# A decoder layer on one core: the MLP's order planned anew, result tiles stored by fewer DMAs

## The chip, the cores and the metric

The kernel runs on one core of a Trainium2 chip. The metric is device time of one execution in microseconds. Three runs before the change took 558.32, 559.50 and 561.14 us, so the median is 559.5 us. The core's engines are TensorE (PE, with its weight loads as PEld), VectorE (DVE), ScalarE (ACT), GpSimd (POOL) and SyncE (SP, which here issues nearly all DMAs). Each engine takes its instructions strictly in the order of the program.

## The reference, cut to what matters

One decoder layer over 512 tokens of width 1024, in float32:

```
xn   = rms_norm(h, g_mix_norm);  proj = xn @ w_in
attn = moba_attention(q, k, v);  conv = conformer_conv(u, ...)
h    = h + concat(attn, conv) @ w_out
hn   = rms_norm(h, g_mlp_norm)
ff   = square(relu(hn @ w_mlp_in))       # 1024 -> 4096
h    = h + ff @ w_mlp_out                # 4096 -> 1024
out  = rms_norm(h, g_final)
```

The change concerns the last four lines: the MLP and the final norm.

## The kernel before, in words

TensorE keeps float32 accuracy by splitting both operands into a high part (rounded, on ACT) and a low part (the rest, `x - high`, a subtraction on DVE or POOL), and multiplying three times: high*high, high*low, low*high (`mm3`, L268 to L270).

The MLP runs in four chunks (c = 0 to 3) of 1024 hidden columns. A chunk has two phases.

- *Hidden phase*: eight blocks of 24 matmuls (`hidden`, tile `ff`). Each needs a 128x1024 tile of w1, loaded as `raw`, and split into `wh` (ACT) and `wl` (kind `mw`). The result goes through `relu_square` (ACT makes `rl`, DVE makes `F`).
- *Product phase*: the second matrix product is done by Strassen's scheme: seven products of half-size blocks instead of eight, in the order 3, 6, 4, 2, 1, 5, 7 (`spread`, `product`, tiles `m`; 24 matmuls each, in two halves j = 0 and 1). Each product needs an operand `O[m]` made of `F` (a sum or difference into a `temp`, kind `ms`, then high part `ma..h` on ACT and low part `mal`), and two weight tiles `B[m]` made of w2 blocks (a sum or difference, kind `mt`, into a tile `t` or `r`, then `wh`, and `wl` of kind `mb`). Product 1's weights are built in place in the tiles of product 2's (`s1 = sums("mt1", r11, ...)` needs `low_of(2)`): the sum for product 1 can start only when the low part of product 2's weights has been taken. Each product is added from PSUM to the residual `xr` by DVE (`add_to`, L1092), up to four 128x512 additions a product.

The sums, differences and low parts are all 128x1024 operations with two inputs in SBUF (L1058, L1066). A chunk has 44 of them: 8 `mw`, 14 `mb`, 10 `mt`, 7 `mal`, 5 `ms`. The table `ON` says on which engines each kind may stand; a kind that is not in it may stand on either.

At the end each of four 128-token tiles is normed: ACT squares and sums, POOL does the small scalar steps and the power (`fr`), one half of the tile is multiplied by g_fin first and scaled later (`mfo`, `mfy`), the other in one operation (`mfz`), and each half is stored by its own DMA from SP.

The order on each engine is not written by hand. Class `Plan` simulates the engines with costs in us, and at each turn emits the step that can start first, with a bias by kind (`BIAS`) between steps that are about even. It has one `port` that POOL operations and DVE operations marked `shared` (two SBUF inputs) hold in turn: such a step is taken to start only when the port is free.

Of the kernel before, what the change touches and what calls it, by code (L numbers as in the profile page):

```python
# [13 lines left out]
AF = mybir.ActivationFunctionType  # L14
# [22 lines left out]
    "mal": ("dve",), "ms1": ("dve",), "ms5": ("dve",), "ms6": ("dve",), "ms7": ("pool",), "mt1": ("pool",),  # L37
    "mt3": ("pool",), "mt6": ("pool",), "mt7": ("dve",),
# [31 lines left out]
class Plan:  # L70
# [32 lines left out]
    def run(self):  # L103
# [8 lines left out]
        while ready:  # L112
            best, first = [], {}
            for s in ready:
# [56 lines left out]
def hybrid_layer(ctx: ExitStack, tc: tile.TileContext, x, pack, w_in, w_out, g_mlp, w1, w2, g_fin, out):  # L171
# [882 lines left out]
    def low_parts(kind, lo, x, hi, needs, uses):  # L1054
# [5 lines left out]
        l = plan.step(kind, either(kind), 0, fn, needs=needs, uses=uses, shared=True)  # L1060
        return l

    def combine(kind, out, a, b, op, needs, uses):
# [84 lines left out]

    def final_ssq(t, cols, ready, half, final):
# [7 lines left out]

# [247 lines left out]
```

## Time and profile before

| | |
|---|---|
| median of three runs | 559.5 us |
| profiled execution | 559.28 us, of which the traced span is 557.5 us |
| PE busy | 540.6 us (97% of the span) |
| DVE, ACT, POOL busy | 444.1, 296.6, 228.7 us |
| granted TensorE clock, mean | 0.991 of 2.4 GHz |
| hidden phases of chunks 0 to 3 begin | 218.6, 302.3, 384.2, 466.0 us |

The span runs from the first to the last instruction; the rest of the 559.28 us (1.8 us) lies around it. Busy shares are averages over stages; where an engine works without a gap, as PE does over most of the span, it sets the time, and another engine matters there only when it makes that engine wait.

### The profile page before, as it was taken

Reading aid. Unit: us, or ns where it says so; the run is one execution under the profiler, and the core shown is the slowest. Engines: PE = TensorE matmul, PEld = TensorE weight load, DVE = VectorE, ACT = ScalarE, POOL = GpSimd, SP = SyncE. Lnnn points to the kernel's source line nnn. Section 1 sums busy time; section 2 is a strip of 40 time slices with the busy share of each in tenths; the row PEclk is TensorE's granted clock in tenths of the full one; section 3 lists DMA queues with packets and bytes.
Section 4 is the critical chain, followed back from the end, with each engine's and each line's share of the span. In section 5 each row is a group of like instructions: output and inputs, shape, how many; then the busy total and the mean of one; then the engine's idle time right before and its main releaser. Section 6 shows DMA issues by size and latency. Waiting matters only on the chain.

```text
span 557.5 us, 7335 instructions
## 1 busy us (share of the span) xinstructions
PE 540.6 (97%) x2676; PEld 452.3 (81%) x2676; DVE 444.1 (80%) x603; ACT 296.6 (53%) x465; POOL 228.7 (41%) x196
## 2 busy tenths in 40 slices
PE   7999999899799999999999999999999999999993
PEld 7988888787678888988888888888888888888882
DVE  4479899899998757487999486999475999395996
ACT  6776486989984734343653333553244453245354
POOL 3289988499755511250060610140510230610453
PEclk8999999999999999999999999999999999999997
DMA  8443313130212451460026820028620048520003
GB/s 276 150 123 106 114 38 119 70 85 32 74 59 95 129 174 38 161 217 0 1 75 194 259 77 0 1 79 227 221 76 1 0 115 240 174 76 1 0 2 151
DMA packets 58835, 56.18 MB, mean 101 GB/s; under 512 B 1840, under 2 KB 42928, under 8 KB 58800
## 3 DMA queue, kind: packets, MB, share of 16 engines
q1 hardware_dynamic: 58512, 54.68, 31.5%
q10 hardware_dynamic: 288, 1.05, 0.5%
q8 instruction: 21, 0.34, 0.2%
q14 instruction: 14, 0.11, 0.1%
HBM read 53.62 MB, written 2.10 MB: 100 GB/s over the span
## 4 chain that ended last, share of the span: by engine, by line
PE 91%; DVE 3%; ACT 2%; issue 1%; DMA 1%; POOL 0%; SPq 0%; ACTq 0%; POOLq 0%
PE ff L270 10%; PE ff L269 10%; PE ff L268 10%; PE m L269 9%; PE m L270 9%; PE m L268 9%; PE u L268 3%; PE u L269 3%; PE u L270 3%; PE y L268 3%; PE y L270 3%; PE y L269 3%; PE q L270 1%; PE q L268 1%; PE v L268 1%; PE q L269 1%
## 5 line engine op out<-in xcount | busy, mean ns | idle before, releaser
L268 PE MATMUL ff<-hTh,wh 128*128 128x512 f32 (+1 forms) x280 | 104.0, 371 | 0.0
L269 PE MATMUL ff<-hTl,wh 128*128 128x512 f32 (+1 forms) x280 | 103.9, 371 | 0.0
L270 PE MATMUL ff<-hTh,wl 128*128 128x512 f32 (+1 forms) x280 | 103.9, 371 | 0.0
L1066 POOL TENSOR_TENSOR r<-r,r 128x1024 f32<-128x1024 f32 x16 | 45.3, 2841 | 142.7 <-DVE wl L1058 136.8
L555 POOL TENSOR_TENSOR acc<-acc,ct 128x512 f32<-128x512 f32 x60 | 89.3, 1488 | 11.7 <-ACT ct L552 8.4
L1074 ACT CAST wh<-raw 128x1024 fp32r<-128x1024 f32 x29 | 30.6, 1055 | 79.0 <-PE ff L269 59.0
L1074 ACT CAST wh<-r 128x1024 fp32r<-128x1024 f32 x40 | 41.7, 1051 | 44.7 <-POOL r L1066 25.7
L1058 DVE TENSOR_TENSOR wl<-raw,wh 128x1024 fp32r<-128x1024 f32 x29 | 42.7, 1472 | 26.4 <-ACT wh L1074 26.3
L1092 DVE TENSOR_TENSOR xr<-xr,m 128x512 f32<-128x512 f32 x96 | 59.5, 676 | 0.9 <-PE m L270 0.9
L269 PEld LDWEIGHTS ff<-hTl,wh 128*128 128x128 f32 x280 | 52.8, 188 | 9.1
L268 PEld LDWEIGHTS ff<-hTh,wh 128*128 128x128 f32 x280 | 52.8, 188 | 9.1
L270 PEld LDWEIGHTS ff<-hTh,wl 128*128 128x128 f32 x280 | 52.8, 188 | 9.0
L1066 POOL TENSOR_TENSOR t<-r,r 128x1024 f32<-128x1024 f32 x8 | 20.0, 2505 | 90.1 <-DMA r<-w 89.9
L1058 DVE TENSOR_TENSOR wl<-r,wh 128x1024 fp32r<-128x1024 f32 x38 | 50.3, 1353 | 0.8 <-ACT wh L1074 0.8
L1109 DVE SCALAR_TENSOR_TENSOR F<-ff,rl 128x512 f32<-128x512 f32 x32 | 21.9, 685 | 33.5 <-ACT rl L1108 33.5
L1108 ACT ACTIVATE rl<-ff 128x512 f32<-128x512 f32 x32 | 19.0, 593 | 48.5 <-PE ff L270 48.5
L571 DVE SCALAR_TENSOR_TENSOR cs<-hin,pk,cs 128x512 f32<-128x512 f32 x58 | 43.4, 749 | 0.9
L552 ACT ACTIVATE ct<-hin,pk 128x512 f32<-128x512 f32 x60 | 40.5, 718 | 2.5 <-POOL acc L555 1.7
L458 ACT CAST wh<-raw 128x1024 fp32r<-128x1024 f32 x21 | 22.1, 1050 | 21.7 <-PE u L269 9.9
L462 DVE TENSOR_TENSOR wl<-raw,wh 128x1024 fp32r<-128x1024 f32 x20 | 30.1, 1507 | 1.8 <-ACT wh L458 1.7
L268 PE MATMUL u<-xh,wh 128*128 128x256 f32 (+1 forms) x88 | 29.7, 338 | 0.0
L269 PE MATMUL u<-xl,wh 128*128 128x256 f32 (+1 forms) x88 | 29.4, 334 | 0.0
(224 smaller groups left out, 1360.0 us busy)
## 6 DMA issues: line engine op xcount, KB each, us to landing
raw<-w SPq DMA_DIRECT2D x32, 512.0 KB, 3.9
r<-w SPq DMA_DIRECT2D x32, 512.0 KB, 5.3
raw<-w_in SPq DMA_DIRECT2D x18, 512.0 KB, 3.6
raw<-w_out SPq DMA_DIRECT2D x8, 512.0 KB, 3.7
xr<-x SPq DMA_DIRECT2D x4, 512.0 KB, 5.2
out<-ot SPq DMA_DIRECT2D x8, 256.0 KB, 2.1
x<-x SPq DMA_DIRECT2D x4, 256.0 KB, 4.2
raw<-w_in SPq DMA_DIRECT2D x4, 256.0 KB, 6.0
```

The costliest lines, as they stand in the source:

```text
L268: nc.tensor.matmul(ps, sh, mh, start=first, stop=False)
L269: nc.tensor.matmul(ps, sh, ml, start=False, stop=False)
L270: nc.tensor.matmul(ps, sl, mh, start=False, stop=last)
L458: nc.scalar.copy(hi, raws[n])
L462: e.tensor_tensor(lo, raws[n], f32(hi), op=OP.subtract)
L552: p = plan.step(f"prod{i}", "act", 0.72, lambda src=src, j=j, ct=ct: nc.scalar.activation(get(ct), src, AF.Copy, scale=wtap(i, j)), needs= ...
L555: s = plan.step(f"tapp{i}", "pool", 1.38, lambda ct=ct: nc.gpsimd.tensor_tensor(get(acc), get(acc), get(ct), op=OP.add), needs=[p, s], use ...
L571: s = plan.step(f"tapd{i}", "dve", 0.78, lambda src=src, j=j, last=last: nc.vector.scalar_tensor_tensor(get(acc) if last else get(cs), src ...
L1058: e.tensor_tensor(lo(), x(), f32(hi()), op=OP.subtract)
L1066: e.tensor_tensor(out(), a(), b(), op=op)
L1074: h = plan.step(f"{kind}h", "act", 1.04, lambda: nc.scalar.copy(get(wb)[0], get(b)), needs=[ready, last.get("high")], uses=[b, wb])
L1092: return plan.step("mev", "dve", dve_cost(n), lambda: nc.vector.tensor_tensor(xt[t][:, cols], xt[t][:, cols], get(b)[:, 0:n], op=op), need ...
```

## The change

The places in the code:

```diff
 ON = {
-    "mal": ("dve",), "ms1": ("dve",), "ms5": ("dve",), "ms6": ("dve",), "ms7": ("pool",), "mt1": ("pool",),
-    "mt3": ("pool",), "mt6": ("pool",), "mt7": ("dve",),
+    "mal": ("pool",), "mfo0": ("dve",), "mfo1": ("dve",), "mfo2": ("pool",), "mfo3": ("pool",), "ms5": ("pool",),
+    "ms6": ("pool",), "mt1": ("pool",), "mt4": ("pool",), "mt6": ("pool",), "mwl": ("pool",),
 }
 BIAS = {
...
-    "mfo": -646, "ms1": 261,
+    "mfo": -241, "mfo1": -121, "mfo3": -193, "mfq": -267, "mfq3": -181, "mfz": -398, "ms": 779,
...
-    def __init__(self, clocks):
+    def __init__(self, clocks, port_wait=9.0):
...
-                        a = max(a, self.port)
+                        a = max(a, min(self.port, a + self.port_wait) if e == "dve" else self.port)
...
-                self.port = a + c
+                self.port = max(self.port, a + c)
...
-    plan = Plan({"pe": 0.0, "act": 1.5, "dve": 3.0, "pool": 0.0, "sp": 0.0})
+    plan = Plan({"pe": 0.0, "act": 1.5, "dve": 3.0, "pool": 0.0, "sp": 0.0}, port_wait=0.5)
...
-        last["mfo", t] = plan.step("mfo", "dve", 0.69, lambda: nc.vector.tensor_mul(ot()[:, d], xt[t][:, d], gfi_b["t"][:, d]),
+        def gains():
+            e = nc.gpsimd if o["eng_used"] == "pool" else nc.vector
+            e.tensor_tensor(ot()[:, d], xt[t][:, d], gfi_b["t"][:, d], op=OP.mult)
+        o = last["mfo", t] = plan.step(f"mfo{t}", either(f"mfo{t}", 0.69, 1.38), 0, gains, ...)
...
-                nc.vector.tensor_add(n, ms, msq[t])
+                nc.vector.scalar_tensor_tensor(n, ms, first["ms"][0], msq[t], op0=OP.add, op1=OP.add)
...
-        for s, cols in ((s1, d), (s2, e)):
-            plan.step("mst", "sp", 0.5, lambda cols=cols: nc.sync.dma_start(out[t * P:(t + 1) * P, cols], ot()[:, cols]), ...)
+        if t != 1:
+            plan.step("mst", "sp", 0.5, lambda: nc.sync.dma_start(out[t * P:(t + 1) * P], ot()), needs=[s1, s2], uses=[b])
+            return
+        plan.step("mst", "act", 0.5, lambda: nc.scalar.dma_start(out[t * P:(t + 1) * P, d], ot()[:, d]), ...)
+        plan.step("mst", "sp", 0.5, lambda: nc.sync.dma_start(out[t * P:(t + 1) * P, e], ot()[:, e]), ...)
```

So in the MLP's plan a DVE operation is now taken to wait at most 0.5 us for the port, all low parts of w1 and of the operands go to POOL, and of the final multiplications by g_fin those of tiles 2 and 3 do. Tiles 0, 2 and 3 are stored by one DMA of 512 KB each; tile 1, the last, by two of 256 KB from ACT's and SP's queues. One scalar addition of tile 1 moves from POOL into a DVE operation.

The instructions of PE stand in the same order as before, and up to the MLP those of all engines do. In the MLP the other engines' order changes. First POOL in chunk 1. All that POOL does for this chunk before (`t30`, `t31`: differences for product 3; `r20`, `r21`: sums for product 6; `r1`: the sums for product 1; `temp3`: for product 7):

```order
L1066 TENSOR_TENSOR t30_1_3296<-r20_1_3253,r20_1_3287 128x1024
L1066 TENSOR_TENSOR r20_1_3253<-r20_1_3253,r1_3292 128x1024
L1066 TENSOR_TENSOR t31_1_3363<-r21_1_3294,r21_1_3329 128x1024
L1066 TENSOR_TENSOR r21_1_3294<-r21_1_3294,r1_3333 128x1024
L1066 TENSOR_TENSOR r1_3292<-r1_3292,r20_1_3287 128x1024
L1066 TENSOR_TENSOR r1_3333<-r1_3333,r21_1_3329 128x1024
L1066 TENSOR_TENSOR temp3_3410<-F1_1_3441 128x1024
```

And POOL in chunk 1 now, the twelve operations of the end of the hidden phase and of the products (`op..`: low parts of the operands of products 3, 6, 4, 2, then 1, 5, 7; the two `r1` sums for product 1 stand eighth and ninth here):

```order
L1068 TENSOR_TENSOR t40_1_3440<-r1_3391,r1_3288 128x1024
L1068 TENSOR_TENSOR t41_1_3467<-r1_3404,r1_3329 128x1024
L1060 TENSOR_TENSOR opxh_3400<-F0_1_3284,opxh_3400 128x1024
L1060 TENSOR_TENSOR opxh_3400<-temp3_3402,opxh_3400 128x1024
L1060 TENSOR_TENSOR opxl_3534<-F1_1_3436,opxl_3534 128x1024
L1060 TENSOR_TENSOR opxl_3534<-temp2_3532,opxl_3534 128x1024
L1068 TENSOR_TENSOR temp2_3532<-F0_1_3284,F1_1_3436 128x1024
L1068 TENSOR_TENSOR r1_3288<-r1_3288,r20_1_3286 128x1024
L1068 TENSOR_TENSOR r1_3329<-r1_3329,r21_1_3326 128x1024
L1060 TENSOR_TENSOR opffh_3554<-temp3_3402,opffh_3554 128x1024
L1060 TENSOR_TENSOR opffh_3554<-temp2_3532,opffh_3554 128x1024
L1060 TENSOR_TENSOR opffl1_3700<-temp3_3402,opffl0_3699 128x1024
```

Ahead of these the chunk has eleven more (eight `wl`, two `r2`, one `temp3`), so POOL goes from 7 to 23 of the chunk's 44 operations, and DVE from 37 to 21.

Second, DVE in chunk 1, in the product phase. Before, from the last low part for product 6 (`wl_3533`) on; `wl_3581` and `wl_3614` are the low parts of product 2's weights, for which the two `r1` sums on POOL wait. Two more additions follow these rows, then `wl_3653`, the first low part for product 1:

```order
L1058 TENSOR_TENSOR wl_3533<-r21_1_3294,wh_3532 128x1024
L1066 TENSOR_TENSOR temp2_3551<-F0_1_3290,F1_1_3441 128x1024
L1058 TENSOR_TENSOR wl_3554<-t40_1_3406,wh_3553 128x1024
L1058 TENSOR_TENSOR wl_3576<-t41_1_3476,wh_3575 128x1024
L1058 TENSOR_TENSOR opffh_3556<-temp3_3410,opffh_3556 128x1024
L1058 TENSOR_TENSOR wl_3581<-r1_3292,wh_3580 128x1024
L1058 TENSOR_TENSOR wl_3614<-r1_3333,wh_3613 128x1024
L1092 TENSOR_TENSOR xr_1978<-xr_1978,m310_3516 128x512
L1092 TENSOR_TENSOR xr_1978<-xr_1978,m311_3520 128x512
L1092 TENSOR_TENSOR xr_1978<-xr_1978,m310_3516 128x512
L1092 TENSOR_TENSOR xr_1978<-xr_1978,m311_3520 128x512
L1092 TENSOR_TENSOR xr_1978<-xr_1978,m610_3561 128x512
```

And now, from the first operation after the chunk's last `F`; `wl_3590` and `wl_3611` are here product 2's. Four more additions follow, then `wl_3649`, the first for product 1:

```order
L1068 TENSOR_TENSOR temp2_3532<-F0_1_3284,F1_1_3436 128x1024
L1068 TENSOR_TENSOR temp3_3402<-F0_1_3284,F1_1_3436 128x1024
L1060 TENSOR_TENSOR wl_3529<-r21_1_3318,wh_3528 128x1024
L1060 TENSOR_TENSOR wl_3550<-t40_1_3440,wh_3549 128x1024
L1094 TENSOR_TENSOR xr_1978<-xr_1978,m310_3512 128x512
L1060 TENSOR_TENSOR wl_3572<-t41_1_3467,wh_3571 128x1024
L1094 TENSOR_TENSOR xr_1978<-xr_1978,m311_3516 128x512
L1094 TENSOR_TENSOR xr_1978<-xr_1978,m310_3512 128x512
L1060 TENSOR_TENSOR wl_3590<-r1_3288,wh_3589 128x1024
L1094 TENSOR_TENSOR xr_1978<-xr_1978,m311_3516 128x512
L1060 TENSOR_TENSOR wl_3611<-r1_3329,wh_3610 128x1024
L1094 TENSOR_TENSOR xr_1978<-xr_1978,m610_3557 128x512
```

Between the last `F` and the low parts of product 2's weights DVE had ten operations of 128x1024 before (five of them ahead of the rows shown: two `temp` and three low parts); it has five now, and three additions stand among them, while POOL has three operations in the same stretch (`opxl`, `opxl`, `temp2`) in place of none.

Third, DVE at the end of the kernel. Before (`m730`, `m731`, `mlast`: product 7; `ot1` holds tiles 2 and 3, `ot0` tiles 0 and 1; `fr2`: the norm's factor of tile 2):

```order
L1092 TENSOR_TENSOR xr_1978<-xr_1978,m730_4950 128x512
L1145 TENSOR_TENSOR ot1_4989<-xr_1978,gfinbc_2733 128x512
L1092 TENSOR_TENSOR xr_1978<-xr_1978,m731_4982 128x256
L1145 TENSOR_TENSOR ot1_4989<-xr_1978,gfinbc_2733 128x512
L1179 SCALAR_TENSOR_TENSOR ot1_4989<-xr_1978,fr3_2538,gfinbc_2733 128x512
L1092 TENSOR_TENSOR xr_1978<-xr_1978,mlast_5006 128x256
L1145 TENSOR_TENSOR ot0_5036<-xr_1978,gfinbc_2733 128x512
L1166 SCALAR_TENSOR_TENSOR fs1_256_5040,ms_f1_256_5039<-xr_1978 128x256
L1168 TENSOR_TENSOR fn1_256_2542<-ms_f1_256_5039,fn1_0_2541 128x1
L1145 TENSOR_TENSOR ot0_5036<-xr_1978,gfinbc_2733 128x512
L1179 SCALAR_TENSOR_TENSOR ot0_5036<-xr_1978,fr0_2540,gfinbc_2733 128x512
L1179 SCALAR_TENSOR_TENSOR ot0_5036<-xr_1978,fr1_2543,gfinbc_2733 128x512
```

And now:

```order
L1094 TENSOR_TENSOR xr_1978<-xr_1978,m730_4956 128x512
L1149 TENSOR_TENSOR ot0_5003<-xr_1978,gfinbc_2697 128x512
L1094 TENSOR_TENSOR xr_1978<-xr_1978,m731_4981 128x256
L1149 TENSOR_TENSOR ot0_5003<-xr_1978,gfinbc_2697 128x512
L1094 TENSOR_TENSOR xr_1978<-xr_1978,mlast_5008 128x256
L1193 SCALAR_TENSOR_TENSOR ot1_4889<-xr_1978,fr2_4965,gfinbc_2697 128x512
L1177 SCALAR_TENSOR_TENSOR fs1_256_5036,ms_f1_256_5035<-xr_1978 128x256
L1179 SCALAR_TENSOR_TENSOR fn1_256_2539<-ms_f1_256_5035,ms_f1_0_5028,ms0f1_4988 128x1
L1193 SCALAR_TENSOR_TENSOR ot1_4889<-xr_1978,fr3_5001,gfinbc_2697 128x512
L1193 SCALAR_TENSOR_TENSOR ot0_5003<-xr_1978,fr0_5031,gfinbc_2697 128x512
L1193 SCALAR_TENSOR_TENSOR ot0_5003<-xr_1978,fr1_5043,gfinbc_2697 128x512
```

The multiplications for tiles 0 and 1 stand ahead of the last addition now; the `fr2` operation, which stood ahead of the first of these rows, comes after the last addition.

## Rows read from the trace of the kernel before

**Rows 1.** The page's first part: busy time of each engine (share of span), instructions.

```profile
PE 540.6 (97%) x2676; PEld 452.3 (81%) x2676; DVE 444.1 (80%) x603; ACT 296.6 (53%) x465; POOL 228.7 (41%) x196
```

**Rows 2.** Busy time by stretch, chunk 1: stretch, its length, engines, clock, DMA.

```profile
302.26:384.16 81.90, 81.90 (x361) 67.51 (x360) 65.71 (x71) 33.92 (x37) 19.62 (x7) 1.00 0.34 103
```

**Rows 3.** Who waited for whom, weight loads: us in total, times, longest.

```profile
PEld m L269 <- DVE wl L1058: 1.5, 4, 0.4
```

**Rows 4.** Groups of instructions, POOL, chunk 1: count | busy us, mean ns | idle before.

```profile
L1066 POOL TENSOR_TENSOR t<-r,r 128x1024 f32<-128x1024 f32 x2 | 4.8, 2402 | 24.9 <-DMA r<-w 24.9
```

**Rows 5.** The same of DVE, chunk 1.

```profile
L1058 DVE TENSOR_TENSOR wl<-t,wh 128x1024 fp32r<-128x1024 f32 x4 | 4.8, 1219 | 0.0
```

**Rows 6.** Instructions in order of time, POOL, 311 to 324 us: start, duration.

```profile
314.24 3.44 POOL L1066 TENSOR_TENSOR r<-r,r 128x1024 f32<-128x1024 f32 x1
...
320.44 2.40 POOL L1066 TENSOR_TENSOR r<-r,r 128x1024 f32<-128x1024 f32 x1
```

**Rows 7.** The same of DVE, 311 to 324 us.

```profile
314.20 1.23 DVE L1058 TENSOR_TENSOR wl<-raw,wh 128x1024 fp32r<-128x1024 f32 x1 [3.61 <-ACT wh L1074]
...
320.74 3.18 DVE L1058 TENSOR_TENSOR wl<-raw,wh 128x1024 fp32r<-128x1024 f32 x1
```

**Rows 8.** The same of DVE, chunk 1's product phase.

```profile
346.61 0.69 DVE L1109 SCALAR_TENSOR_TENSOR F<-ff,rl 128x512 f32<-128x512 f32 x1 [3.27 <-ACT rl L1108]
347.34 2.36 DVE L1066 TENSOR_TENSOR temp<-F,F 128x1024 f32<-128x1024 f32 x2
...
358.70 2.35 DVE L1058 TENSOR_TENSOR wl<-r,wh 128x1024 fp32r<-128x1024 f32 x2
360.97 4.26 DVE L1092 TENSOR_TENSOR xr<-xr,m 128x512 f32<-128x512 f32 x7
365.15 1.61 DVE L1058 TENSOR_TENSOR wl<-r,wh 128x1024 fp32r<-128x1024 f32 x1
```

**Rows 9.** The same of POOL, chunk 1's product phase.

```profile
360.06 5.62 POOL L1066 TENSOR_TENSOR r<-r,r 128x1024 f32<-128x1024 f32 x2 [37.23 <-DVE wl L1058]
365.65 3.39 POOL L1066 TENSOR_TENSOR temp<-F 128x1024 f32<-128x1024 f32 x1
```

**Rows 10.** The same of ACT, chunk 1's product phase.

```profile
347.42 1.05 ACT L1082 CAST opxl<-F 128x1024 fp32r<-128x1024 f32 x1
...
363.35 1.05 ACT L1074 CAST wh<-r 128x1024 fp32r<-128x1024 f32 x1 [5.09 <-POOL r L1066]
```

**Rows 11.** The same of PE: the first matmul of product 1, chunk 1.

```profile
367.84 0.39 PE L268 MATMUL m<-wh,opffh 128*128 128x512 f32 x1
```

**Rows 12.** The same of PE: the kernel's last matmul.

```profile
548.08 0.28 PE L270 MATMUL mlast<-wh,opffl 128*128 128x256 f32 x1
```

**Rows 13.** The same of DVE, the end.

```profile
545.65 0.74 DVE L1179 SCALAR_TENSOR_TENSOR ot<-xr,fr,gfinbc 128x512 f32<-128x512 f32 x1
...
549.11 0.41 DVE L1092 TENSOR_TENSOR xr<-xr,mlast 128x256 f32<-128x256 f32 x1
...
550.04 0.42 DVE L1166 SCALAR_TENSOR_TENSOR fs<-xr 128x256 f32<-128x256 f32 x1
...
551.25 1.41 DVE L1179 SCALAR_TENSOR_TENSOR ot<-xr,fr,gfinbc 128x512 f32<-128x512 f32 x2
```

**Rows 14.** The same of POOL, the end.

```profile
544.62 0.55 POOL L1177 TENSOR_TENSOR fr<-fn,mhalf 128x1 f32<-128x1 f32 x1
```

**Rows 15.** The same of SP's queue, the end: eight stores are issued.

```profile
546.42 7.57 SPq L1184 DMA_DIRECT2D out<-ot  x8
```

**Rows 16.** DMA throughput from 546 to 557.5 us in 40 slices of 0.29 us.

```profile
GB/s 0 0 0 0 185 420 306 0 0 0 0 164 427 321 299 420 378 427 299 0 0 0 0 0 242 378 435 378 435 378 420 406 399 178 0 0 0 0 0 0
```

**Rows 17.** Busy time by stretch, three early stretches; columns as in rows 2.

```profile
4.30:7.71 3.41, 1.42 (x12) 0.98 (x10) 1.66 (x4) 2.16 (x6) 0.26 (x1) 1.00 0.89 249
7.71:11.13 3.42, 3.42 (x16) 3.12 (x17) 1.26 (x3) 1.93 (x6) 1.87 (x3) 0.50 1.12 337
...
106.69:110.10 3.41, 1.96 (x9) 1.16 (x7) 1.89 (x5) 3.35 (x7) 0.37 (x1) 1.00 0.43 150
```

More of the change, by code (lines that the diff above doesn't have):

```diff
@@ L1001, in hybrid_layer, with either @@
     NCH = DFF // P // CHUNK
-    def either(kind):
-        costs = {"dve": 1.23, "pool": 2.45}
+    def either(kind, *us):
+        costs = dict(zip(("dve", "pool"), us))
         return {e: costs[e] for e in ON.get(kind, costs)}
-    plan = Plan({"pe": 0.0, "act": 1.5, "dve": 3.0, "pool": 0.0, "sp": 0.0})
+    plan = Plan({"pe": 0.0, "act": 1.5, "dve": 3.0, "pool": 0.0, "sp": 0.0}, port_wait=0.5)
     plan.slots("ps", [], 0.0)
@@ L1058, in fn @@
             e.tensor_tensor(lo(), x(), f32(hi()), op=OP.subtract)
-        l = plan.step(kind, either(kind), 0, fn, needs=needs, uses=uses, shared=True)
+        l = plan.step(kind, either(kind, 1.23, 2.45), 0, fn, needs=needs, uses=uses, shared=True)
         return l
@@ L1066, in fn @@
             e.tensor_tensor(out(), a(), b(), op=op)
-        s = plan.step(kind, either(kind), 0, fn, needs=needs, uses=uses, shared=True)
+        s = plan.step(kind, either(kind, 1.23, 2.45), 0, fn, needs=needs, uses=uses, shared=True)
         return s
@@ L1088, in pe_step, with add_to @@
         return last["pe"]
-    def add_to(t, cols, b, needs, op=OP.add):
+    def add_to(t, cols, b, needs, op=OP.add, kind="mev"):
         n = cols.stop - cols.start
-        return plan.step("mev", "dve", dve_cost(n), lambda: nc.vector.tensor_tensor(
+        return plan.step(kind, "dve", dve_cost(n), lambda: nc.vector.tensor_tensor(
             xt[t][:, cols], xt[t][:, cols], get(b)[:, 0:n], op=op), needs=needs, uses=[b])
@@ L1135, in final_half @@
         junk = new_rl(f"fj{t}")
-        s = plan.step("mfa", "act", 0.85, lambda: msq.__setitem__(t, mean_square(get(junk), xt[t][:, d], f"f{t}")),
+        s = plan.step(f"mfa{t}", "act", 0.85, lambda: msq.__setitem__(t, mean_square(get(junk), xt[t][:, d], f"f{t}")),
                       needs=ready, uses=[junk])
@@ L1142, in add_eps @@
             msq[t] = m
-        s = plan.step("mfp", "pool", 0.27, add_eps, needs=[s])
-        last["mfo", t] = plan.step("mfo", "dve", 0.69, lambda: nc.vector.tensor_mul(ot()[:, d], xt[t][:, d], gfi_b["t"][:, d]),
-                  needs=ready, uses=[ot_b[t // 2]], shared=True)
+        s = plan.step(f"mfp{t}", "pool", 0.27, add_eps, needs=[s])
+        def gains():
+            e = nc.gpsimd if o["eng_used"] == "pool" else nc.vector
+            e.tensor_tensor(ot()[:, d], xt[t][:, d], gfi_b["t"][:, d], op=OP.mult)
+        o = last["mfo", t] = plan.step(f"mfo{t}", either(f"mfo{t}", 0.69, 1.38), 0, gains, needs=ready, uses=[ot_b[t // 2]], shared=True)
         return s
+    first = {}
     def final_ssq(t, cols, ready, half, final):
@@ L1154, in final_ssq @@
             box = {}
-            s = plan.step("mfs", "act", 0.23 + w / 820, lambda: box.__setitem__(0, mean_square(get(sq)[:, 0:w], xt[t][:, cols], f"f{t}_{cols.start}")),
+            s = plan.step(f"mfs{t}", "act", 0.23 + w / 820, lambda: box.__setitem__(0, mean_square(get(sq)[:, 0:w], xt[t][:, cols], f"f{t}_{cols.start}")),
                           needs=ready, uses=[sq])
+            if t == 1:
+                first["ms"] = box
+                return s
             def add():
@@ L1160, in add @@
                 msq[t] = n
-            s = plan.step("mfq", "pool", 0.27, add, needs=[s, half])
+            s = plan.step(f"mfq{t}", "pool", 0.27, add, needs=[s, half])
         else:
@@ L1167, in both @@
                                                accum_out=ms)
-                nc.vector.tensor_add(n, ms, msq[t])
+                nc.vector.scalar_tensor_tensor(n, ms, first["ms"][0], msq[t], op0=OP.add, op1=OP.add)
                 msq[t] = n
-            s = plan.step("mfd", "dve", 0.7, both, needs=list(ready) + [half], uses=[sq], shared=True)
+            s = plan.step("mfd", "dve", 0.7, both, needs=list(ready) + half, uses=[sq], shared=True)
         return s
@@ L1344, in chunk @@
         s = product(7, banks, tiles=(0,))
[L1345 removed]
+        s = add_to(0, D1, banks[0], [s] + done[0, 0], kind="mev0")
         final_store(0, D2, final_ssq(0, D1, [s], half[0], True), otile[0])
@@ L1350, in chunk @@
             s = product(7, {1: ps}, tiles=(1,), cols=cols)
-            s = add_to(1, cols, ps, [s] + done[1, 0])
-            half[1] = final_ssq(1, cols, [s], half[1], n == 1)
+            s = add_to(1, cols, ps, [s] + done[1, 0], kind="mev1")
+            half[1] = final_ssq(1, cols, [s], half[1], n == 1) if n else [half[1], final_ssq(1, cols, [s], None, False)]
         final_store(1, D2, half[1], otile[1])
```

20 lines of the change are left out of this document (11 added, 9 removed), and 11 rows, old and new, of the table BIAS.

## The prediction

> **What bounds the kernel now.** I read the busy times first, then the busy time of one MLP chunk, then the waits of the weight loads, and last the instructions in order of time. PE is busy 97% of the span [rows 1]. In chunk 1 of the MLP it is busy for all of its 81.90 us, at full clock [rows 2]. In the whole MLP the only wait of a weight load that recurs is for a DVE low part: four times, 1.5 us together, one a chunk [rows 3]. So an MLP that feeds PE better can give back 1.5 us at most; one that feeds it worse costs every microsecond by which a matmul is late, since PE has no gap in which to make it up. The other part that the change can shorten lies behind the last matmul: it ends at 548.36 [rows 12], the profiled execution lasts 559.28 us, so 10.9 us.
>
> DVE has 65.71 us of work in chunk 1 and POOL 19.62 [rows 2]; from that view there is room to move work to POOL. The view that decides is another one: whether the two can work at once. A POOL difference of 128x1024 takes 2.40 us undisturbed [rows 4], a DVE low part 1.22 [rows 5]. At 314.24 a POOL sum took 3.44: a DVE low part had started at 314.20 and ended at 315.43, and 2.40 us back from POOL's end at 317.68 is 315.28 [rows 6, 7]. At 320.74 a DVE low part took 3.18: POOL's sum held on until 322.84, and 1.22 back from DVE's end at 323.92 is 322.70. So neither starts before the other has ended (the handover is 0.14 us ahead of the recorded end). The additions `xr<-xr,m`, which read PSUM, are free of this: seven of them take 4.26 us, 0.60 each, beside POOL's sums [rows 8, 9]. Where both queues ask, they take turns: DVE's low part at 365.15 gets its turn when POOL's sum ends at 365.68, and POOL's next operation, ready at 365.65, waits behind it and takes 3.39 [rows 8, 9].
>
> The change's plan goes by another price, at most 0.5 us of waiting for DVE. The Trainium skill, page "SBUF — State Buffer", section "Who interferes with whom", says that a DVE instruction with two SBUF inputs and a GpSimd instruction that reads SBUF shut each other out for the whole instruction. By that the 1.96 us of waiting at 320.74 is the ordinary case, and by 0.5 us the sum below would have no stall.
>
> **The change part by part.**
>
> *Port time.* A chunk has 44 operations that take turns. Before, 7 on POOL and 37 on DVE: 7 x 2.40 + 37 x 1.22 = 61.9 us. Now 23 on POOL and 21 on DVE: 23 x 2.40 + 21 x 1.22 = 80.8 of the chunk's 81.9 us. DVE's own load falls, but the pair's is now as long as PE's, and the work comes in bursts.
>
> *The product phase.* I walk through chunk 1 on the clock of before, with the new order, 2.40 and 1.22 us an operation, 0.14 us of overlap at each handover, 0.60 for an addition. The last `F` ends at 347.30 [rows 8]. DVE makes `temp2` and, right behind it, `temp3`, as before [rows 8], until 349.70; POOL's low part of operand 4 needs a cast that ends at 348.47 [rows 10], so it comes after `temp3` (either may win). From here turns: POOL operand 4 until 351.95; DVE `wl_3529` until 353.05; POOL operand 2 until 355.3; DVE `wl_3550` until 356.4; POOL `temp2` until 358.65; DVE meanwhile one addition, then `wl_3572` until 359.75, two additions, and product 2's first low part `wl_3590` until 362.1. Before, its counterpart began at 358.70 and ended at 359.9 [rows 8]: 2.2 us late. Now the chain for product 1: POOL's first `r1` sum 362.2 to 364.6; DVE's `wl_3611`, asked for in between, runs 364.45 to 365.65; POOL's second `r1` sum until 368.1, where before both had ended by 365.68 [rows 9]. ACT's cast takes 1.05 [rows 10] from 364.65. DVE has five additions, until 368.7, and then asks for `wl_3649`; POOL has begun the low part of operand 1 at 368.1 and holds on until 370.5; `wl_3649` runs until 371.6. Product 1's first matmul stood at 367.84 [rows 11], so it is 3.8 us late. Its second half: POOL's operand 5 takes 371.5 to 373.9, DVE's `wl_3667`, asked for at 372.2, ends at 375.0, and is due 12 matmuls after 371.6, at 374.4 with 81.90/361 = 0.227 us each [rows 2]: 0.6 late. Products 5 and 7 follow on time. Together 4.4 us a chunk, and smaller stalls ahead of it (products 4 and 2) are contained in it.
>
> Each chunk has the same order in this phase, and PE has no slack to regain it: 4 x 4.4 = 17.6 us. Bounds: nothing, if the turns fall so that DVE wins each of them; 2 x 2.27 more a chunk if POOL gets one turn twice in a row at two places. The nearest rows, 314.24, 320.74 and 365.15, all show turns, so I take 4.4.
>
> *The last chunk's product 5.* In the last chunk DVE's order has an addition, `temp3` and three additions between product 1's second low part and product 5's first, in the others none of these. 375.0 + 0.6 + 1.14 + 1.8 + 1.2 = 379.8 on the same clock, due at 374.4 + 0.6 + 12 x 0.227 = 377.7: 2.1 us. Bounds 0 and 3.1 (one more turn of POOL).
>
> *Hidden phase.* Eight low parts of w1 go to POOL, 2.40 us each, while PE needs one each 5.44 us (24 x 0.227): the cover is wide, cost nothing; if one came a turn late (1.22) it would still be in time. The load of g_fin moves a few places ahead on ACT's queue; it is used at the end alone and costs nothing.
>
> *The end.* Multiplications by g_fin for tiles 2 and 3 on POOL lie beside product matmuls; if operand 7, queued behind the first of them, came late, one POOL operation, 2.4 us, is the price; I take 0 and keep it for the range. Behind the last matmul (E = 548.36): before, the last addition began at 549.11, E + 0.75, behind an `ot` operation, and DVE's last `ot` ended at 552.66, E + 4.30 [rows 13]. Now nothing holds the addition: E + 0.05 to 0.4; `ot` of tile 2 (0.74) until 1.1; `fs` and `fn` until 1.7; `ot` of tile 3 until 2.4 while the power (0.55 [rows 14]) waits for the port until 2.8; `ot` of tile 0 waits for that and ends at 3.4, of tile 1 at 4.1. So DVE gains 0.2. But the first store was issued at 546.42 [rows 15], before E, because tile 2's `ot` ran at 545.65 [rows 13]; now that operation stands behind the last addition, and all 2.1 MB start after E + 1.1. At about 400 GB/s in dense slices [rows 16] that is 5.2 us; with 0.9 us from issue to the first data (546.42 to about 547.3 in the same view) the data ends at E + 7.2. Before, it ended at 546 + 34 x 0.2875 = 555.8 [rows 16], E + 7.4. I take -0.2; bounds -1.2 (stores no longer than DVE's gain allows) and +1.0 (a gap between stores). Fewer DMAs save only SP's issue time, which is no longer the limit.
>
> **Sum.** 17.6 + 2.1 - 0.2 = 19.5 us on the profiled 559.28 us: 578.8; the median is 0.2 above the profiled execution, 579.0. What the walk leaves out (hops between engines, casts that come late) only lengthens it, by some 0.5 us a chunk as I judge; I predict 581 us.
>
> **The rivals.**
>
> *The clock falls too.* PE would stand still for about 4 us in each chunk. After the stretch 4.30 to 7.71, in which PE was busy for 1.42 us, the granted clock was 0.50 (1.2 of 2.4 GHz) for 3.42 us; after 106.69 to 110.10, with 1.96 us busy, it stayed at 1.00 [rows 17]. A half clock for 3.42 us after each long stall loses 1.7 us, four times 6.8: 581 + 6.8 = 588. For it: a 4 us stall is longer than any in this MLP. Against it: part of the loss returns, as the low parts get ahead while PE is slow, and the stall may come in two pieces. The Trainium skill, page "TensorE: Matmul & The Clock Gate", section "HAM oscillation — how this bites in real kernels", describes a loop in which each wait for data sends the next group of matmuls to the half rate; by it this rival is the expected case.
>
> *Turns fall better.* If DVE's first two turns come ahead of POOL, half the lateness goes: 4 x 2.2 + 2.1 - 0.2 = 10.7, 570 us. For it: the first race, at 348.5, is about even.
>
> *Not slower: the plan's 0.5 us holds.* The waits in rows 7 would be chance, PE is fed throughout, its 1.5 us of waits go and 0.2 at the end: 557.8 us. It decides where DVE's waits stay so short that the 3.8 us go: five of them lie on the path to product 1 (`wl_3529`, `wl_3550`, `wl_3572`, `wl_3611`, `wl_3649`), of 1.8 to 2.3 us each, so at about 1.3 us or less each. Against it stand the rows at 314.24 and 320.74, which show no sharing of any kind.
>
> **How the numbers follow.** Forecast (575 to 585): 0.55. Clock: 0.22. Better turns: 0.09. Not slower: 0.12. Left over, 0.02, a late operand 7 or worse. The range takes in the forecast, the clock's 588 with a late operand 7 (590), and the better turns down to 568: 568 to 590 holds about 0.85. A change under 0.5% (2.8 us) can't be told from none here; the not-slower case is worth 1.7 us, so most of its chance is "same": faster 0.03, same 0.09, slower 0.88.
>
> **What would show it.** Right: PE waits for DVE `wl` at product 1 of each chunk, some 3 to 4 us; DVE low parts with means near 2 us in the product phase; POOL near 60 us busy a chunk; a chunk of about 86 us; the first store after the last matmul. Wrong: chunks of 82 us, or POOL and DVE operations that overlap at full speed. A granted clock of 0.50 inside the MLP would show the first rival.

## The result, and the profile after

The changed kernel takes 583.39 us (median of 6 runs, 580.20 to 584.46), the one before 559.94 (6 runs): a ratio of 1.0416 with a 95% interval of 1.0393 to 1.0438. It is slower by 23.5 us; forecast was 581 us. The profiled execution took 582.07 us, its span 580.4. Medians and ratios in this document leave out one execution, of 583.48 us, which lay over 1.5% above the fastest of its kernel.

The first part of the page, to be held against [rows 1]:

```profile
PE 549.6 (95%) x2676; PEld 455.6 (79%) x2676; DVE 444.8 (77%) x542; ACT 295.6 (51%) x465; POOL 393.8 (68%) x256
```

DVE has 61 instructions fewer and yet the same busy time as before (444.1 us): what was taken off it came back as waiting inside its instructions. The chain of work that ended last names what PE waited for. By engine before, then by engine and by line now; DVE's share went from 3% to 19%:

```profile
PE 91%; DVE 3%; ACT 2%; issue 1%; DMA 1%; POOL 0%; SPq 0%; ACTq 0%; POOLq 0%
```

```profile
PE 65%; DVE 19%; issue 7%; POOL 3%; ACT 2%; DMA 2%; SPq 0%; DVEq 0%; POOLq 0%; ACTq 0%
DVE wl L1060 9%; PE ff L272 8%; PE ff L270 8%; PE ff L271 8%; DVE xr L1094 5%; PE m L271 3%; PE m L272 3%; PE m L270 3%; PE u L270 3%; PE u L271 3%; PE u L272 3%; PE y L270 3%; PE y L272 3%; PE y L271 3%; PE q L272 1%
```

The waits, weight loads and matmuls (columns as in [rows 3], where it was 1.5 us):

```profile
PEld m L271 <- DVE wl L1060: 21.1, 17, 3.3
...
PE m L271 <- DVE wl L1060: 13.9, 12, 2.9
```

Chunk 1 by stretch, and four stretches that are read further down (columns as in [rows 2]):

```profile
311.09:397.23 86.14, 82.82 (x361) 67.26 (x360) 62.14 (x50) 33.51 (x37) 62.59 (x24) 1.00 0.30 92
290.72:294.13 3.41, 0.90 (x4) 0.77 (x5) 3.41 (x3) 2.02 (x3) 3.41 (x2) 1.00 0.00 0
294.13:297.54 3.41, 3.41 (x10) 2.66 (x9) 3.41 (x2) 0.00 (x0) 1.28 (x1) 0.50 0.55 154
376.05:379.46 3.41, 1.48 (x7) 0.90 (x5) 3.41 (x4) 2.49 (x3) 3.41 (x3) 1.00 0.00 0
379.46:382.88 3.42, 2.49 (x11) 2.07 (x12) 3.42 (x3) 0.45 (x1) 3.13 (x1) 1.00 0.30 84
```

86.14 us where [rows 2] had 81.90. The low parts of chunk 1 on DVE, by form, show the inside of it: 2.4 to 2.5 us each, against 1.219 in [rows 5]; and on POOL 2.9 to 3.4 us against 2.402 in [rows 4]:

```profile
L1060 DVE TENSOR_TENSOR wl<-r,wh 128x1024 fp32r<-128x1024 f32 x10 | 23.8, 2392 | 0.0
...
L1060 DVE TENSOR_TENSOR wl<-t,wh 128x1024 fp32r<-128x1024 f32 x4 | 10.1, 2532 | 0.5 <-ACT wh L1076 0.5
```

```profile
L1060 POOL TENSOR_TENSOR opffh<-temp,opffh 128x1024 fp32r<-128x1024 f32 x2 | 5.7, 2868 | 0.0
L1060 POOL TENSOR_TENSOR opxl<-F,opxl 128x1024 fp32r<-128x1024 f32 x1 | 3.4, 3411 | 4.6 <-ACT opxl L1084 4.6
```

The place where PE stands still, in order of time: DVE, then POOL, then PE (compare [rows 8, 9, 11]).

```profile
371.43 3.03 DVE L1060 TENSOR_TENSOR wl<-r,wh 128x1024 fp32r<-128x1024 f32 x1
374.38 3.07 DVE L1094 TENSOR_TENSOR xr<-xr,m 128x512 f32<-128x512 f32 x5
377.37 2.97 DVE L1060 TENSOR_TENSOR wl<-r,wh 128x1024 fp32r<-128x1024 f32 x1
```

```profile
370.98 2.40 POOL L1068 TENSOR_TENSOR r<-r,r 128x1024 f32<-128x1024 f32 x1 [3.49 <-DVE wl L1060]
374.54 2.40 POOL L1068 TENSOR_TENSOR r<-r,r 128x1024 f32<-128x1024 f32 x1 [1.16 <-DVE wl L1060]
376.89 5.70 POOL L1060 TENSOR_TENSOR opffh<-temp,opffh 128x1024 fp32r<-128x1024 f32 x2
```

```profile
377.14 0.39 PE L270 MATMUL m<-wh,opffh 128*128 128x512 f32 x1
380.39 0.50 PE L271 MATMUL m<-wl,opffh 128*128 128x512 f32 x1 [2.87 <-DVE wl L1060]
```

DVE makes its five additions while POOL does the second `r1` sum; 0.48 us before DVE asks for product 1's low part, POOL has begun the low part of operand 1. DVE's instruction lasts until 380.34, PE's next matmul starts at 380.39: 3.25 us after the one before, where 0.227 is the normal step, so 3.03 us are lost. POOL itself wasn't what came late: ahead of both `r1` sums it stood idle until DVE had made a low part of product 2 (3.49 and 1.16 us).

By chunk, from the first matmul of each hidden phase to the next, last column to the end of the last matmul:

| | start | chunk 0 | 1 | 2 | 3 | behind the last matmul |
|---|---|---|---|---|---|---|
| before | 218.56 | 83.70 | 81.90 | 81.87 | 82.33 | 9.13 |
| after | 220.13 | 90.96 | 86.14 | 86.17 | 88.38 | 8.57 |
| difference | +1.57 | +7.26 | +4.24 | +4.30 | +6.05 | -0.56 |

The sum is the 22.9 us between the spans. The 1.57 lies where the order is the same in both; two kernels further down with the same instructions up to there (`end_only` and `price_only`) start chunk 0 at 218.34 and 220.11, so it is within what runs differ by. The end: last matmul, DVE's last operations, SP and ACT's queue:

```profile
571.50 0.28 PE L272 MATMUL mlast<-wh,opffl 128*128 128x256 f32 x1
```

```profile
571.82 0.42 DVE L1094 TENSOR_TENSOR xr<-xr,mlast 128x256 f32<-128x256 f32 x1 [0.39 <-PE mlast L272]
...
573.53 2.07 DVE L1193 SCALAR_TENSOR_TENSOR ot<-xr,fr,gfinbc 128x512 f32<-128x512 f32 x3
```

```profile
572.97 2.36 SPq L1198 DMA_DIRECT2D out<-ot  x3
575.62 0.33 SPq L1201 DMA_DIRECT2D out<-ot  x1
```

The addition no longer waits for another operation of DVE, all stores start behind the last matmul (E = 571.78), and DVE is done at E + 3.82, 0.5 us earlier than before.

### The profile page after: what moved, and what is told of

The parts are those of the page before. It is cut to its first block, busy times and chain, and to the rows that moved or that the text cites. A ratio compares the mean times of both kernels' runs of the same rounds, so it can differ in the third digit from the quotient of the medians.

```text
span 580.4 us, 7344 instructions
## 1 busy us (share of the span) xinstructions
PE 549.6 (95%) x2676; PEld 455.6 (79%) x2676; DVE 444.8 (77%) x542; ACT 295.6 (51%) x465; POOL 393.8 (68%) x256
## 4 chain that ended last, share of the span: by engine, by line
PE 65%; DVE 19%; issue 7%; POOL 3%; ACT 2%; DMA 2%; SPq 0%; DVEq 0%; POOLq 0%; ACTq 0%
DVE wl L1060 9%; PE ff L272 8%; PE ff L270 8%; PE ff L271 8%; DVE xr L1094 5%; PE m L271 3%; PE m L272 3%; PE m L270 3%; PE u L270 3%; PE u L271 3%; PE u L272 3%; PE y L270 3%; PE y L272 3%; PE y L271 3%; PE q L272 1%
## 5 line engine op out<-in xcount | busy, mean ns | idle before, releaser
L1060 POOL TENSOR_TENSOR wl<-raw,wh 128x1024 fp32r<-128x1024 f32 x29 | 75.6, 2612 | 32.6 <-ACT wh L1076 32.6
L1060 DVE TENSOR_TENSOR wl<-r,wh 128x1024 fp32r<-128x1024 f32 x40 | 86.1, 2162 | 0.0
L1068 POOL TENSOR_TENSOR r<-r,r 128x1024 f32<-128x1024 f32 x16 | 38.4, 2401 | 20.9 <-DVE wl L1060 18.6
L1060 DVE TENSOR_TENSOR wl<-t,wh 128x1024 fp32r<-128x1024 f32 x16 | 45.8, 2865 | 1.2 <-ACT wh L1076 1.2
L1068 DVE TENSOR_TENSOR t<-r,r 128x1024 f32<-128x1024 f32 x8 | 16.3, 2035 | 30.7 <-DMA r<-w 30.7
L271 PE MATMUL m<-wl,opffh 128*128 128x512 f32 x64 | 27.0, 422 | 12.8 <-DVE wl L1060 12.8
L464 DVE TENSOR_TENSOR wl<-raw,wh 128x1024 fp32r<-128x1024 f32 x20 | 30.2, 1510 | 1.8 <-ACT wh L460 1.7
```

Source lines behind the costliest of these rows:

```text
L271: nc.tensor.matmul(ps, sh, ml, start=False, stop=False)
L464: e.tensor_tensor(lo, raws[n], f32(hi), op=OP.subtract)
L1060: e.tensor_tensor(lo(), x(), f32(hi()), op=OP.subtract)
L1068: e.tensor_tensor(out(), a(), b(), op=op)
```

## The experiments

The theory: DVE's and POOL's operations with SBUF inputs take turns, and on the way to product 1 the turns add up until its low part is late. Rivals: the changed store order, the plan's price for the port alone, POOL being slow by itself, or only the one POOL operation that stands beside product 1's low part. All ratios are to the kernel before, run on the same chip.

**POOL as busy, without the port.** The order stays; the operands' low parts on POOL become memsets of the same length together (0.96 + 0.96 + 0.53 us). The values of these low parts are left out of the computation.

```diff
-            e.tensor_tensor(lo(), x(), f32(hi()), op=OP.subtract)
+            if kind == "mal" and l["eng_used"] == "pool":
+                for rows in (4, 4, 2):
+                    e.memset(f32(lo())[:, 0:rows], 0.0)
+                return
+            e.tensor_tensor(lo(), x(), f32(hi()), op=OP.subtract)
```

> The changed kernel, same order on every engine, but the seven low parts of the operands a chunk are not computed on POOL: three memsets of the same tile (1024 + 1024 + 512 columns) stand in their place, which leave the low parts of the operands at zero. By POOL's small memsets (128x128 in 0.2 us, 128x30 in 0.12) they should keep POOL about 2.4 us, but they read no SBUF. If DVE waits because POOL's low parts hold a read port, DVE's low parts in the product phase fall back to about 1.2 us, PE waits under 1 us a chunk, a chunk takes 82 us: 557 to 561 us. If the cause were that POOL is occupied (its own results come late), or the order of DVE and ACT by itself, PE keeps its 3.3 us wait at product 1: 575 us or more.

Measured: 558.12 us, ratio 0.9977 (0.9960 to 0.9993). Chunk 1 takes 81.60 us, and POOL is busy for 57.09 of them. At the place above POOL works without a gap, and beside it DVE's low part takes 1.22. Stretch, POOL at an earlier place and at this one, DVE:

```profile
302.19:383.79 81.60, 81.60 (x362) 67.58 (x360) 51.19 (x54) 33.84 (x37) 57.09 (x38) 1.00 0.34 104
```

```profile
342.11 5.04 POOL L1062 MEMSET opxl<- 128x1024 f32 x6
...
363.56 5.05 POOL L1062 MEMSET opffh<- 128x1024 f32 x6
```

```profile
364.05 1.22 DVE L1064 TENSOR_TENSOR wl<-r,wh 128x1024 fp32r<-128x1024 f32 x1
```

Without the reads of the operands' seven low parts a chunk all of the loss is gone: PE waits nowhere in the product phases. The edit does one thing more, since a memset needs no input: POOL writes the low parts of operands 4 and 2 already 39.9 us into the chunk (342.11), where the subtractions began 46.3 us in. So this run alone doesn't part turns from a POOL that is merely late. Two rows do: at 364.05 the low part falls from 2.97 to 1.22 us beside a busy POOL, and in the changed kernel POOL waited for DVE ahead of the `r1` sums (370.98, 374.54). The 1.22 us beside memsets, for 2.97 beside subtractions, agree with the Trainium skill, page "SBUF — State Buffer", section "Who interferes with whom": a two-input DVE instruction contends with a GpSimd instruction that reads SBUF, not with one that only writes it.

**Neighbour or sum of turns?** The same edit for the low parts of operands 1 and 5 alone, which stand beside product 1's (`l["m"] in (1, 5)`), and for the other five alone (`(2, 3, 4, 6, 7)`), with the values left out likewise.

> The changed kernel, with the low parts of operands 1 and 5 alone (both on POOL, issued right beside product 1's own low parts on DVE) written as three memsets of about the same length on POOL; the values of these low parts are left out of the computation, the order stays. If lateness adds up over all the turns of the product phase (the prediction's walk): product 1's wl starts where it started (377.37 in chunk 1 of the changed kernel) but takes 1.2 instead of 2.97, so the wait of 3.03 falls to about 1.3, the second half's wait stays between 0 and 1.2; about 1 to 2 us a chunk comes back and with shorter waits the half-clock stretches (1.6 us each, two of them) go: 570 to 576 us. If the loss is made only by the operation that stands beside product 1's low part: 3.5 us a chunk and the clock come back, 562 to 566.

> The counterpart: the low parts of operands 2, 3, 4, 6 and 7 written as memsets, those of 1 and 5 left on POOL beside product 1's low parts as in the changed kernel. If lateness adds up over all turns: the chain of sums and low parts ahead of product 1 runs earlier by two to three turns of 1.2 to 2.4 us, product 1's low part is asked for before operand 1's takes the port or soon after it ends, and the wait of 3.03 falls below 1: 559 to 565 us. If only the neighbour counts: nothing changes at product 1, 578 to 583.

Measured: 570.87 us, ratio 1.0205 (1.0182 to 1.0229), without the neighbours; 561.18, ratio 1.0030 (1.0015 to 1.0046), without the others. So taking away the neighbours gives back 12.5 us, and taking away the turns of the others 22.2; that is more than 23.5 together, so each part costs most of its price only on top of the other. Without the neighbours PE in chunk 1 still waits, 374.09 - 372.59 - 0.23 = 1.27 us, for a low part that DVE starts as late in the chunk as in the changed kernel (66.3 us in), then for a memset:

```profile
374.09 0.50 PE L271 MATMUL m<-wl,opffh 128*128 128x512 f32 x1 [1.11 <-DVE wl L1064]
374.92 0.50 PE L272 MATMUL m<-wh,opffh 128*128 128x512 f32 x1 [0.33 <-POOL opffh L1062]
```

Without the others the collision is there in full, on DVE, then POOL, and PE doesn't notice:

```profile
366.50 3.04 DVE L1064 TENSOR_TENSOR wl<-r,wh 128x1024 fp32r<-128x1024 f32 x1
```

```profile
366.03 5.77 POOL L1064 TENSOR_TENSOR opffh<-temp,opffh 128x1024 fp32r<-128x1024 f32 x2
```

```profile
369.93 0.39 PE L270 MATMUL m<-wh,opffh 128*128 128x512 f32 x1
370.16 0.39 PE L271 MATMUL m<-wl,opffh 128*128 128x512 f32 x1
```

The two meet as before, 0.47 us apart (0.48 above), and the low part again takes 3 us; but DVE asks for it 4.4 us earlier in the chunk, and it ends at 369.54, before the matmul at 370.16 needs the tile. The loss is the sum of turns, as the walk had it; the rival that the one neighbour makes it alone falls.

**Low parts of operands back on DVE**, the rest as changed.

```diff
-    "mal": ("pool",),
+    "mal": ("dve",),
```

> The changed kernel with only the low parts of the operands put back on DVE (POOL 16 of a chunk's 44 operations), then planned anew with the changed biases. If those seven operations are the ones that cost: PE's 3.3 us wait at product 1 goes; what stays is the biases' part, a wait at product 6: 565 to 573 us. If the low parts of w1 (eight, in the hidden phase) cost as much: 575 us or more.

Measured: 577.00 us, ratio 1.0309 (1.0276 to 1.0343), above what was expected. The wait at product 1 falls to 0.5 us. The time is that of the other branch, but not for its reason: PE waits nowhere for a low part of w1. A new wait, from 358.52 to 361.12, less 0.23: 2.37 us, stands at product 6 in chunk 1, although POOL has 229 instructions for 256. One POOL operation makes most of it (3.40 - 1.22 = 2.18); DVE, then POOL:

```profile
356.52 1.22 DVE L1060 TENSOR_TENSOR opffh<-temp,opffh 128x1024 fp32r<-128x1024 f32 x1
357.65 3.40 DVE L1060 TENSOR_TENSOR wl<-r,wh 128x1024 fp32r<-128x1024 f32 x1
```

```profile
356.68 3.29 POOL L1068 TENSOR_TENSOR temp<-F,F 128x1024 f32<-128x1024 f32 x1 [14.33 <-DVE opxl L1060]
```

**The price of the port, the table of engines, the biases.** Four edits of the changed kernel: (a) the price of before; (b) the table of before, with g_fin's products of tiles 2 and 3 left on POOL; (a) with (b); (c) the biases of before. The fifth has table and biases of before with the new price and the new end.

```diff
(a)
-    plan = Plan({...}, port_wait=0.5)
+    plan = Plan({...}, port_wait=9.0)
(b)
-    "mal": ("pool",), ... "mt4": ("pool",), "mt6": ("pool",), "mwl": ("pool",),
+    "mal": ("dve",), "ms1": ("dve",), ... "mt3": ("pool",), "mt6": ("pool",), "mt7": ("dve",),
(c)
-    "mal": -321, ... "mbh": -689, "mbl": -352, "mev": -339, "mfo": -241, ... "ms": 779,
+    "mbh": -377, "mbl": -249.6, "mev": -240.1, "mfo": -646, "ms1": 261,
```

> The changed kernel with one number undone: the MLP's plan again takes a DVE operation to wait for the whole POOL operation (9.0 in place of 0.5). The table still puts 23 of a chunk's 44 operations on POOL. Theory of the port's load (80.8 us of port time in a chunk of 82): knowing the wait does not remove it, 576 to 585 us. Rival, the plan's wrong price is the cause: the plan now steers round the waits, 558 to 564 us.

> The changed kernel with the table of engines of before (POOL 7 or 8 of a chunk's 44 operations), biases, price and end as changed. If POOL's share alone makes the loss: 557 to 562 us. Rival, the new biases alone also cost: in the new order the low part for product 6's second half stands on DVE behind two temps, three low parts of operands, one temp (6 x 1.14 us) and one POOL operation that holds the port (up to 2.1): from 347.3 it ends near 357.5, due at 353.9, 3.6 us late a chunk, 14 us in all: about 573 us, with one PE wait of 3 to 4 us a chunk at product 6 and none at product 1.

> The earlier run with before's table of engines and the new biases, now with the price of before (DVE waits until POOL has ended). If the new biases alone make the order in which product 6's low part comes last on DVE: as that run, 573 to 583. If it took price and biases together: 558 to 563.

> The changed kernel with the table of engines as changed (low parts of operands and of some weights on POOL) and the biases of the kernel before: the mirror image of the run that had the new biases with the old table. If POOL's share of the operations that take turns is enough by itself, whatever the order: 576 to 590. If the new biases carried most of the loss: under 568.

> The kernel before with its table of engines and its biases, the end of the changed kernel, and the plan's price for a shared port as changed (DVE waits at most 0.5 us). If the wrong price makes the loss, DVE's low parts get planned beside POOL's sums and PE waits as in the changed kernel: over 570. If the order that table and biases make carries it, the plan has few places where the price decides and PE stays fed: 558 to 562.

Measured, with the next section's `end_only` in the first row:

| table | biases | price as changed | price of before |
|---|---|---|---|
| before | before | 559.57, 0.9997 (0.9980 to 1.0014) | 559.84, 1.0010 (0.9992 to 1.0028) |
| before | new | 580.86, 1.0352 (1.0282 to 1.0421) | 579.99, 1.0353 (1.0324 to 1.0381) |
| new | before | 590.20, 1.0543 (1.0512 to 1.0575) | not run |
| new | new | 583.39, 1.0416 (1.0393 to 1.0438) | 580.27, 1.0366 (1.0338 to 1.0395) |

The price costs nothing by itself, and with the new biases alone nothing that the ratios show (1.0352 and 1.0353); with table and biases it is 3.1 us, where the two intervals just touch. So the wrong price isn't the cause. Table and biases each cost 20 to 31 us alone (590.20 is 0.2 above what was expected), and together no more than that. That the biases alone cost so much was not expected: POOL has the share of before then (228.4 us). DVE, POOL and PE of the run with the old table and the new price, and last the same matmul with the price of before:

```profile
359.36 1.22 DVE L1068 TENSOR_TENSOR temp<-F,F 128x1024 f32<-128x1024 f32 x1
360.50 3.38 DVE L1060 TENSOR_TENSOR wl<-r,wh 128x1024 fp32r<-128x1024 f32 x1
```

```profile
359.53 3.27 POOL L1068 TENSOR_TENSOR temp<-F 128x1024 f32<-128x1024 f32 x1 [28.57 <-DVE opffh L1060]
```

```profile
360.29 0.39 PE L270 MATMUL m<-wh,opxh 128*128 128x512 f32 x1
363.93 0.80 PE L271 MATMUL m<-wl,opxh 128*128 128x512 f32 x1 [3.26 <-DVE wl L1060]
```

```profile
362.13 0.80 PE L271 MATMUL m<-wl,opxh 128*128 128x512 f32 x1 [3.26 <-DVE wl L1060]
```

The low part at 360.50 is product 6's last. In the order of before it stands ahead of the `temp` that is at 359.36 here (the second piece on DVE in the section on the change). Behind it, it starts 1.14 us later and, what is worse, after POOL's `temp` has begun at 359.53, which costs another 2.16 (3.38 - 1.22): 3.3 us, and PE waits 3.41. Both runs have this wait in all four chunks. So by these traces one misplaced row of DVE's order, made by the biases and met by a single POOL operation, costs about as much as the sixteen operations that the table moves; no run put back that row alone. With the new table and the old biases PE waits at product 1 for ACT's casts of the late `r1` sums as well:

```profile
PEld m L270 <- DVE wl L1059: 13.6, 11, 3.4
PEld m L269 <- ACT wh L1075: 12.8, 4, 3.3
```

The old-table run lies above what was expected (about 573), and its times go with the clock: its execution of 574.53 us has a mean clock of 0.992, those of 580.86 and 582.25 have 0.983 and 0.982. In the profiled one (583.48 us, 0.977) the granted clock falls to 0.50 (1.2 of 2.4 GHz) after the wait in each chunk; in chunk 1:

```profile
360.23:363.64 3.41, 0.44 (x2) 0.02 (x1) 3.41 (x2) 1.99 (x2) 2.57 (x1) 1.00 0.00 0
363.64:367.05 3.41, 3.12 (x7) 2.51 (x8) 3.41 (x4) 0.00 (x0) 0.00 (x0) 0.50 0.00 0
```

**The end.** The new end with before's tables and price; the changed kernel with eight half-tile stores from SP as before; and a version meant to beat both kernels: the first of these with a few changed entries.

```diff
(the stores)
-        if t != 1:
-            plan.step("mst", "sp", ...)
...
+        for s, cols in ((s1, d), (s2, e)):
+            plan.step("mst", "sp", 0.5, lambda cols=cols: nc.sync.dma_start(out[t * P:(t + 1) * P, cols], ot()[:, cols]), ...)
(the version meant to beat both)
-    "mt6": ("pool",), "mfo3": ("dve",),
+    "mt6": ("dve",), "mfo3": ("pool",),
...
+    "mt4": 60, "mt6": 150, "mfp": -150,
```

> The kernel before with the tables, the price of a shared port and so the order of the MLP as before, and only the end of the changed kernel (its sums of squares and its five stores). PE must be fed as before; the prediction priced the end at -0.2 us (bounds -1.2 and +1.0): 558 to 561. If part of the loss sits in the new end, it is slower by over 2 us.

> The changed kernel with its eight half-tile stores from SP's queue, as before, in place of five. The loss is in the product phase, so 583 within 1.5 us either way; if the fewer, larger stores had cost or saved more than that, it shows as a difference beyond it.

> The version with before's MLP order and the changed end, with three small edits: tile 3's product with g_fin on POOL (under the last products), the weights' sum of product 6 on DVE instead of POOL, and three biases that fit them. DVE's last operations are shorter by one multiplication of 0.7 us and the four waits of 0.3 to 0.4 us for a low part stay. Expected 1 to 3 us below the kernel before, 556 to 559; if the multiplication on POOL shuts DVE out at the end, as POOL did in the product phase, nothing or a loss of up to 2 us.

Measured: 559.84 us, ratio 1.0010 (0.9992 to 1.0028); 582.08, 1.0424 (1.0366 to 1.0481); and 558.66, 0.9982 (0.9967 to 0.9997). In time of execution neither the stores nor the new sums of squares show a cost or a gain. The traces show one of the stores: with eight of them, the order of operations on DVE, ACT and POOL being the same, SP's first store starts at 569.50, 3.3 us ahead of the last matmul's end (572.81), and 7.60 us lie behind that end, for 8.57 with five:

```profile
569.50 7.82 SPq L1198 DMA_DIRECT2D out<-ot  x8
```

A store of a whole tile waits for its later half; as two stores, the earlier half leaves at once. So the five stores cost about 1.0 us, less than the times of whole executions can tell.

The third is the fastest that computes everything, by 0.9 us: less than the 1 to 3 that were expected, and under the 0.5% that counts as a change here. In its trace the stores start before the last matmul has ended (550.45), and 7.79 us lie behind it, for 9.13 in the kernel before; SP's queue:

```profile
549.12 4.67 SPq L1198 DMA_DIRECT2D out<-ot  x3
554.62 0.33 SPq L1201 DMA_DIRECT2D out<-ot  x1
```

## Why the prediction was right

*Turns.* Shown by the low parts beside POOL's operations and by the memset run. The order of the turns is the walk's. POOL is busy 62.6 us in chunk 1 ("near 60" was written), the waits inside its instructions counted in.

*Product 1.* The walk had its low part end at 371.6 on the clock of before. It ended at 380.34, less the 8.83 us by which chunk 1 starts later, 371.51; POOL's low part of operand 1 was to end at 370.5 and did at 376.89 + 2.37 (the first of the two in its row) - 8.83 = 370.43. Foreseen were 4.4 us a chunk; the two chunks with nothing else in them lost 4.24 and 4.30. In chunk 1 this is 0.27 at product 2, 3.03 at product 1, 0.47 at its second half, and 0.11 for each of several slower first steps behind a wait. (A slip of 0.1 us stands in the walk: 371.6 + 12 x 0.227 is 374.3, not 374.4.)

*The last chunk's product 5.* The term that was mis-sized: 2.1 us foreseen, 1.03 - 0.23 = 0.80 measured:

```profile
560.68 0.50 PE L271 MATMUL m<-wl,opffh 128*128 128x512 f32 x1 [0.65 <-DVE wl L1060]
```

The order of additions that the step spoke of is there, but PE had run at half clock ahead of it, which gave DVE time to catch up. That this is the whole reason isn't shown. With the clock up, in the run without the other five operands' low parts, the same wait is 541.19 - 539.16 - 0.23 = 1.80:

```profile
539.16 0.39 PE L270 MATMUL m<-wh,opffh 128*128 128x512 f32 x1
541.19 0.50 PE L271 MATMUL m<-wl,opffh 128*128 128x512 f32 x1 [1.64 <-DVE wl L1064]
```

*The hidden phase* costs nothing, as foreseen: no matmul waits for a low part of w1. *What the walk left out* was put at 2 us; chunk 0 alone lost 2.9 us more than 4.4. Of these 0.70 is a transpose of `hn` that waits for DVE at 227.18, at the start of the chunk (the memset run has it too), and 1.0 that products 4 and 2 wait three times there, 1.28 us together, where chunk 1 has 0.27. The rest is the first rival's.

*The first rival, the clock,* is true for two chunks of four. After the wait at product 1 the granted clock is 0.50 for one stretch (294.13 above) in chunks 0 and 3, at 1.00 in chunks 1 and 2. A matmul step there:

```profile
294.35 0.63 PE L272 MATMUL m<-wh,opffh 128*128 128x512 f32 x1
294.78 0.63 PE L270 MATMUL m<-wh,opffh 128*128 128x512 f32 x1
```

0.43 us where 0.227 is normal, eight of them, so 1.6 us (1.7 was estimated), of which some returns: the 0.47 at the second half of product 1 is not there in these chunks. What stays can be read where the order is the same and the clock isn't: the run with eight stores has the half clock in chunk 2 too, and that chunk takes 87.20 us, not 86.17. So a fall costs about 1.0 us. Two such stretches were less than the four that this rival needed for 588.

*The end* gave back 0.56, for 0.2 foreseen within -1.2 to +1.0, and the first store left 1.2 us behind the last matmul, for 1.1. The three kernels with memsets, whose order on DVE is the same, have the same figure (8.56 to 8.57 us); with this end and other orders it is -2.2 to +0.5, so it hangs on the order. The prediction put the late first store down to tile 2's `ot` alone; with eight stores that `ot` stands where it stood, and the first store is early. The whole-tile stores have their part in it.

*The sum:* 17.6 + 2.1 - 0.2 + 2 = 21.5 us foreseen. Measured 7.26 + 4.24 + 4.30 + 6.05 - 0.56 = 21.3, and 1.6 ahead of the MLP. That the two meet within 0.2 us is in part luck: product 5 came 1.3 short and the end 0.4, and the two falls of the clock, which the sum left to a rival, made good for it.

*Where the reasoning was too narrow:* it put the loss down to POOL's new share. The runs show that the new biases cost as much with the old share. *The rival "not slower"* is out: beside POOL's operations the low parts above take 2.97 to 3.40 us, 1.8 to 2.2 more than alone, and not 0.5. *Better turns* is out too: the order of the turns was the walk's.

## What to carry to other kernels

Look at two engines that shut each other out as one resource, and follow it up to each instruction that the busiest engine waits for: a low share of time tells little, since one 2.4 us operation of the slower engine, begun just before an urgent one of the faster, cost it 2.2 us here. Put the urgent operation ahead on its own queue, and move to the slower engine what is not followed by anything urgent, or what doesn't take the shared resource. And when weights of a scheduler are changed along with what it schedules, test them apart.

## What was not expected of the hardware

- Five larger stores leave 1.0 us more behind the last matmul than eight smaller ones (8.57 and 7.60 us), with the same order of operations on DVE, ACT and POOL.
- The same wait of 3.03 us was followed by the half clock in two chunks and not in the two others. In the stretch ahead of the fall PE had been busy for 0.90 of 3.41 us (290.72), and for 0.44 in the old-table run (360.23); where the clock stayed, for 1.48 and 2.49 us in the two stretches that the wait touched (376.05, 379.46). Even the wait of 2.4 us at product 6, with the operands' low parts on DVE, was followed by it in one chunk of four.
- The scatter between executions of the changed kernel went with the clock: 580.20 us at a mean clock of 0.989 to 584.46 at 0.984. The memset run, without the waits, scatters less: 557.50 to 559.50 us.
